# The first head pair of the prompt's attention goes ahead in the scheduler's order; batch 0's last two key pages move to other buffers

## The chip, the cores and the metric

One NeuronCore of one Trainium2 chip runs the whole program. The metric is device time in microseconds, the median of three runs. Engines are named as in the profile: PE (TensorE matmul), PEld (its weight load), DVE (VectorE), ACT (ScalarE), POOL (GpSimd) and SP (SyncE). SP, ACT and POOL also issue DMAs.

## What is computed

One inference step of one decoder layer, for a prompt of 512 tokens and for a sample group of 8 sequences of 4 tokens, all in float32:

```python
z  = RMSNorm(x) @ W_in            # columns: RWKV-7 group | FoX attention group | conv group
x += concat(RWKV7(z_A), FoX(z_B), Conv(z_C)) @ W_out
x += CrossAttn(RMSNorm(x), memory K/V)
x += ConvGLU_FFN(RMSNorm(x))
```

Two parts of it meet in the change. **FoX attention of the prompt**, 8 heads of 64, causal:

```python
s = q @ k.T * scale + c[:, None] - c[None, :]     # c: cumulative log forget gates
p = softmax(where(kpos <= qpos, s, -inf));  o = p @ v
```

**FoX attention of the sample**: each of the 8 sequences attends to 2048 cached positions, in 16 pages of 128 that a page table scatters over a pool, plus its own 4 tokens. Keys and values of all heads of one sequence are 8 MB, which the kernel reads by indirect DMAs.

## The kernel before

The program is written in a framework that schedules it: the Python code yields instructions in a program order, every instruction has a priority (its place in that order, moved ahead by `tc.high_priority(n)` by n places), and the scheduler picks, for each engine, the ready instruction with the best priority by its own model of time. What comes out is a fixed queue for each engine, worked off in order on the chip. Tiles come from pools; a pool with n buffers hands out a buffer when the earlier user of it is done, and pools that are opened after others are closed lie on the same storage.

The stage around the change begins at some 306 us, when the last matmul of the input projection is done, and ends at some 634 us, when the cross attention's first matmul starts. Two streams are woven in program order (line 1757), each with a weight that says how fast it advances:

- `sample_past`: for each of the 8 sequences `past_scores(b)` takes four key parts of 1 MB ("pages" below: 128 partitions of 2048 values). Each is loaded by one indirect DMA issued on POOL's queue (line 1292), transposed on DVE (line 1434, `KT`), and multiplied in 32 small matmuls into `bank_s`. After four of them a softmax follows on DVE and ACT. Two sequences later `past_values(b)` takes four value parts of 1 MB.
- `rest`: what is left of the RWKV recurrence, `recurrence_end`, then `prompt_attention` woven with `side_work` (`memory_norm`, `conv_module`), then `memory` (the prompt's memory keys and values, weights `w_xk` and `w_xv`) and `out_prompt` (the output projection).

Key pages live in the pool `wraw` (two buffers, tile `w_raw`), value pages in the pool `fpg` (three buffers, tile `page`). `memory_norm` also takes two tiles from `fpg` (`gain, more = page(), page()`, line 1510). Its first row block uses half of `more` as scratch, its second is loaded into the other half. `fpg` lies on the storage that the input projection's activations held until then.

Batch 0's first two key pages are fetched early, before the stage (lines 1300 and 1301, list `first_keys`). The other two are fetched by `past_scores(0)` when a buffer of `wraw` is free, that is after the first and the second transpose.

`attend(j)` (line 1365) does one pair of heads. For each of four row blocks i it forms scores of both heads in two PSUM banks (three banks `bank_r` go around), adds the causal mask `tri` and takes the minimum on DVE (line 1359, into `S0` and `S1`), and takes the exponential on ACT (line 1381). Then come transposes of `S`, the values' matmuls and the scaling (line 1403), which is the last step of a pair. `tri` is made in `recurrence_end` (lines 1355 and 1356) with its ordinary priority. `tri`, `S0` and `S1` lie in a pool `at` that is opened when the recurrence's storage has been given back; eight stores of the sample's RWKV state (line 1117, from the recurrence's `S0`, issued by SP) still read some of that storage.

`urgent(steps, ahead)` (line 350) runs every step of a stream with `tc.high_priority(ahead)`.

Of the kernel before, what the change touches and what calls it, by code (L numbers as in the profile page):

```python
# [154 lines left out]
def hybrid_step(tc, A):  # L155
# [3 lines left out]
    def pool(name, bufs=1, stack=es, right=False, **kw):  # L159
        return stack.enter_context(tc.tile_pool(name=name, bufs=bufs, side="right" if right else "left", reuse_waits="tile", **kw))  # L160
# [15 lines left out]
    def acopy(out, in_):  # L176
        nc.scalar.copy(out, in_)  # L177
# [7 lines left out]
    def mm(out, lhsT, rhs, start=True, stop=True):  # L185
        pinned(nc.tensor.matmul(out, lhsT, rhs, start=start, stop=stop, skip_group_check=True))  # L186
# [27 lines left out]
    def tr(out, in_, p0=0):  # L214
        k = in_.shape[0]
        pinned(nc.tensor.transpose(out=out, in_=in_, identity=ident[p0:p0 + k, p0:p0 + k]))  # L216
# [133 lines left out]
    def urgent(steps, ahead):  # L350

        while True:
            with tc.high_priority(ahead):
                step = next(steps, None)
            if step is None:
                return
            yield step
# [6 lines left out]
    pg = pool("pg", 2, psA, space=PSUM)  # L364
# [11 lines left out]
    def xb():  # L376
        return px.tile([128, 512], F32, name="bank_x")
# [912 lines left out]
    def four_pages(t, cache, b, pg):  # L1290

        nc.gpsimd.indirect_dma_start(out=t, out_offset=None, in_=A[cache][0].rearrange("n (k j) h d -> (n k) (j h d)", j=4),
                                     in_offset=bass.IndirectOffsetOnAxis(ap=kidx[:, 4 * b + pg: 4 * b + pg + 1], axis=0),
                                     bounds_check=32 * NPHYS - 1, oob_is_err=True)
        return t
# [4 lines left out]
    with tc.high_priority(1500):  # L1300
        first_keys = [four_pages(wraw.tile([128, 2048], F32, name="w_raw"), "cache_fox_k", 0, pg) for pg in range(2)]
# [56 lines left out]
    def add_min(out, a, b, least):  # L1358
        nc.vector.tensor_tensor_reduce(out=out, in0=a, in1=b, scale=1.0, scalar=3e38, op0=ADD, op1=MINO, accum_out=least)
# [5 lines left out]
    def attend(j):  # L1365
        q, k = yF[:, j], kF[:, j]
        st = at2.tile([128, 2, 3, 4], F32, name="st")

        S = [at.tile([128, OFF[4]], F32, name=f"S{r}") for r in range(2)]
        for i in range(4):  # L1370
            n = 128 * (i + 1)
            two = [xb() for _ in range(2)]
            for ps, ro in zip(two, HALF):
                mm(ps[:, :n], q[ro, i * 128: (i + 1) * 128], k[ro, :n], True, False)
            for r, ps in enumerate(two):
                co = slice(64 * r, 64 * r + 40)
                mm(ps[:, :n], e8[co, 2 * j + r: 2 * j + r + 1].broadcast_to([40, 128]), cum[co, :n], False, True)
            for r, ps in enumerate(two):
                o = S[r][:, OFF[i]: OFF[i] + n]
                add_min(o, ps[:, :n], tri[:, SEQ - n:], st[:, r, 0, i: i + 1])  # L1380
                act(out=o, in_=o, func=AF.Exp, scale=-1.0, bias=st[:, r, 0, i: i + 1], accum_out=st[:, r, 1, i: i + 1])
            yield 0.35 * (i + 1) + 0.4
        nc.vector.reciprocal(st[:, :, 2], st[:, :, 1])
        PT = [at.tile([128, OFK[4]], F32, name=f"PT{r}") for r in range(2)]
        for kb in range(4):
            for r in range(2):
                ps = xb()
                for i in range(kb, 4):
                    tr(ps[:, (i - kb) * 128: (i - kb + 1) * 128], S[r][:, OFF[i] + kb * 128: OFF[i] + (kb + 1) * 128])
                anycp(PT[r][:, OFK[kb]: OFK[kb + 1]], ps[:, : 512 - 128 * kb])  # L1390
                yield 0.11 * (4 - kb)
        ps = xb()
        for r, ro in enumerate(HALF):
            for i in range(4):
                mm(ps[ro, i * 128: (i + 1) * 128], st[:, r, 2, i: i + 1].broadcast_to([128, 64]), ident)
        yield 0.9
        rinv = at.tile([128, SEQ], F32, name="rinv")
        acopy(rinv, ps)
        ps = xb()
        for kb in range(4):  # L1400
            for r, ro in enumerate(HALF):
                mm(ps[ro, kb * 128:], vF[:, kb, j * 128 + r * 64: j * 128 + (r + 1) * 64], PT[r][:, OFK[kb]: OFK[kb + 1]], kb == 0, kb == 3)
        vtt(out=yF[:, j, :SEQ], in0=ps, in1=rinv, op=MUL)
        yield 2.2
# [11 lines left out]
    def page():  # L1416
        return fpg.tile([128, 2048], F32, name="page")
# [2 lines left out]
    nc.vector.memset(Pn, 0.0)  # L1420
    ysm = fs1.tile([128, 8, NS], F32, name="ysm")

    held = {}
    def past_scores(b):
        g, b4 = b // 4, b % 4
# [73 lines left out]


    def prompt_attention():
        for j in range(4):
            yield from attend(j)


# [102 lines left out]
    def rest():  # L1608
        nonlocal xTs, kTm, vm, bw
        yield from woven((recurrence, 48.0), (conv_work, 48.0))  # L1610
        recurrence_end()
        mk = pool("mk", 1, mks, True)
        kTm = mk.tile([128, 8, NMEM], F32, name="kTm")
        vm = mk.tile([128, 2, D], F32, name="vm")
        mraw = pool("mraw", 2, m2s, True)
        at_once[0] = 1
        for step in woven((prompt_attention(), 42.0), (side_work(), 33.0, 0.1)):
            yield step * 1.44
        ats.close()
        cvs.close()  # L1620
        wsplit[0] = pool("msp", 2, m2s, True)
        wslot[0] = Slots((mraw, 2), (pool("more", 3, m2s, True), 3))
        yield from memory()
        bw = pool("bwb", 2, m2s, True)
        xTs = residual_places()
        for step in out_prompt():
            yield step * 2.16
# [601 lines left out]
```

## Time and profile before

| | |
|---|---|
| median of 3 runs | 1235.73 us (1229.98 to 1239.14) |
| profiled execution, its own time | 1240.32 us |
| its span | 1238.6 us |
| PE busy, PEld busy | 1147.9 us (93%), 988.1 us (80%) |
| DVE, ACT, POOL busy | 809.7 us (65%), 501.0 us (40%), 282.1 us (23%) |
| moved by DMA | 173.81 MB |

The span is the time from the first to the last instruction. Busy shares are means over stages with different limits; what the change can do is read from the stage of 306 to 634 us alone.

### The profile page before, as it was taken

Reading aid. Unit: us, or ns where it says so; the run is one execution under the profiler, and the core shown is the slowest. Engines: PE = TensorE matmul, PEld = TensorE weight load, DVE = VectorE, ACT = ScalarE, POOL = GpSimd, SP = SyncE. Lnnn points to the kernel's source line nnn. Section 1 sums busy time; section 2 is a strip of 40 time slices with the busy share of each in tenths; the row PEclk is TensorE's granted clock in tenths of the full one; section 3 lists DMA queues with packets and bytes.
Section 4 is the critical chain, followed back from the end, with each engine's and each line's share of the span. In section 5 each row is a group of like instructions: output and inputs, shape, how many; then the busy total and the mean of one; then the engine's idle time right before and its main releaser. Section 6 shows DMA issues by size and latency. Waiting matters only on the chain.

```text
span 1238.6 us, 24738 instructions
## 1 busy us (share of the span) xinstructions
PE 1147.9 (93%) x10354; PEld 988.1 (80%) x10354; DVE 809.7 (65%) x1516; ACT 501.0 (40%) x1001; POOL 282.1 (23%) x318
## 2 busy tenths in 40 slices
PE   6889989999589998989989979999999999999997
PEld 6888878787354555965578746999999999999997
DVE  4698999877668666883256855567777326767522
ACT  5454553342255445534343223355444223444321
POOL 1253430033333332212322420021111001111120
PEclk9999989999698998999989989999999999999999
DMA  7221120122886879887435561233231332322241
GB/s 241 62 68 46 60 86 2 45 84 90 297 294 225 347 290 340 311 283 245 178 112 162 182 216 31 87 113 103 69 102 57 88 107 82 102 93 68 80 121 44
DMA packets 125952, 173.81 MB, mean 140 GB/s; under 512 B 9349, under 2 KB 107413, under 8 KB 117640
## 3 DMA queue, kind: packets, MB, share of 16 engines
q1 hardware_dynamic: 84624, 71.29, 18.7%
q0 software_dynamic: 15056, 84.28, 18.6%
q10 hardware_dynamic: 26160, 16.66, 4.8%
q8 instruction: 81, 1.33, 0.5%
q14 instruction: 31, 0.25, 0.1%
HBM read 164.54 MB, written 7.88 MB: 139 GB/s over the span
## 4 chain that ended last, share of the span: by engine, by line
PE 66%; DVE 12%; issue 9%; ACT 6%; DMA 4%; POOL 3%; POOLq 0%; SPq 0%; DVEq 0%; ACTq 0%
PE bank_g L186 39%; PE bank_d L186 7%; PE bank_r L186 7%; PE bank_s L186 4%; PE bank_v L186 3%; PE bank_a L186 2%; PE bank_r L216 2%; DVE w_lo L247 1%; DVE four L891 1%; PE bank_t L216 1%; DMA w_raw<-in_w_xk_dram 1%; DMA page<-in_cache_fox_v_dram,kidx 1%; ACT w_lo L1470 1%; ACT w_hi L177 1%; DMA w_raw<-in_w_in_dram 1%
## 5 line engine op out<-in xcount | busy, mean ns | idle before, releaser
L186 PE MATMUL bank_g<-four,w_hi 128*128 128x272 f32 (+1 forms) x1536 | 278.1, 299 | 0.7 <-DVE xT L1795 0.6
L177 ACT CAST w_hi<-w_raw 128x1024 fp32r<-128x1024 f32 (+3 forms) x149 | 140.5, 946 | 256.2 <-PE bank_g L186 183.6
L186 PEld LDWEIGHTS bank_g<-four,w_hi 128*128 128x128 f32 x1536 | 221.4, 188 | 10.6 <-issue 5.8
L247 DVE TENSOR_TENSOR w_lo<-w_raw,w_hi 128x1024 fp32r<-128x1024 f32 (+3 forms) x149 | 163.5, 1099 | 83.4 <-ACT w_hi L177 79.8
L186 PE MATMUL bank_g<-four,w_lo 128*128 128x272 f32 (+1 forms) x768 | 171.5, 298 | 0.0
L186 PE MATMUL bank_g<-act_h,w_hi 128*128 128x272 f32 (+2 forms) x400 | 123.2, 308 | 7.6 <-ACT w_hi L177 3.7
L186 PEld LDWEIGHTS bank_g<-four,w_lo 128*128 128x128 f32 x768 | 121.9, 189 | 3.1 <-issue 0.6
L186 PE MATMUL bank_g<-act_l,w_hi 128*128 128x272 f32 (+2 forms) x400 | 120.9, 302 | 0.0
L186 PE MATMUL bank_g<-act_h,w_lo 128*128 128x272 f32 (+2 forms) x400 | 120.7, 302 | 0.0
L2140 POOL TENSOR_SCALAR ysm<-HS,vec 128x32 f32<-128x32 f32 x44 | 41.9, 953 | 255.2 <-ACT HS L177 255.2
L186 PEld LDWEIGHTS bank_g<-act_h,w_hi 128*128 128x128 f32 x400 | 78.1, 195 | 12.2 <-ACT w_hi L177 4.1
L1434 DVE STREAM_TRANSPOSE KT<-w_raw 128x2048 f32<-128x2048 f32 x32 | 73.6, 2300 | 11.0 <-DMA w_raw<-in_cache_fox_k_dram,kidx 10.1
L186 PEld LDWEIGHTS bank_g<-act_l,w_hi 128*128 128x128 f32 x400 | 78.2, 195 | 3.2 <-issue 2.3
L186 PEld LDWEIGHTS bank_g<-act_h,w_lo 128*128 128x128 f32 x400 | 77.8, 195 | 3.1 <-issue 1.6
L186 PE MATMUL bank_d<-four,w_hi 128*128 128x272 f32 x384 | 80.0, 304 | 0.0
L186 PE MATMUL bank_g<-in_l,w_hi 128*128 128x272 f32 x352 | 73.4, 290 | 0.0
L186 PE MATMUL bank_g<-in_h,w_hi 128*128 128x272 f32 x352 | 73.4, 290 | 0.0
L186 PE MATMUL bank_g<-in_h,w_lo 128*128 128x272 f32 x352 | 73.2, 289 | 0.0
L186 PEld LDWEIGHTS bank_d<-four,w_hi 128*128 128x128 f32 x384 | 63.4, 197 | 1.1
L2132 DVE TENSOR_TENSOR up<-bank_g,tot 128x544 f32<-128x544 f32 x44 | 31.8, 722 | 44.7 <-PE bank_g L186 44.6
L186 PE MATMUL bank_s<-KT,w_hi 128*32 128x128 f32 x1024 | 43.8, 305 | 17.7 <-DVE mss L234 9.2
L186 PE MATMUL bank_d<-four,w_lo 128*128 128x272 f32 x192 | 57.8, 301 | 0.0
(623 smaller groups left out, 2386.0 us busy)
## 6 DMA issues: line engine op xcount, KB each, us to landing
w_raw<-in_w_up_dram SPq DMA_DIRECT2D x20, 1024.0 KB, 5.2
w_raw<-in_w_down_dram SPq DMA_DIRECT2D x16, 704.0 KB, 4.6
w_raw<-in_w_in_dram SPq DMA_DIRECT2D x10, 1024.0 KB, 10.2
w_raw<-in_cache_mem_k_dram SPq DMA_DIRECT2D x16, 512.0 KB, 4.9
sV<-in_cache_mem_v_dram POOLq DMA_DIRECT2D x12, 512.0 KB, 6.0
w_raw<-in_w_xk_dram ACTq DMA_DIRECT2D x8, 512.0 KB, 16.4
w_raw<-in_w_xv_dram ACTq DMA_DIRECT2D x8, 512.0 KB, 11.6
w_raw<-in_w_out_dram ACTq DMA_DIRECT2D x8, 512.0 KB, 11.1
```

Source lines behind the costliest of these rows:

```text
L177: nc.scalar.copy(out, in_)
L186: pinned(nc.tensor.matmul(out, lhsT, rhs, start=start, stop=stop, skip_group_check=True))
L216: pinned(nc.tensor.transpose(out=out, in_=in_, identity=ident[p0:p0 + k, p0:p0 + k]))
L247: tt(out=l, in0=src, in1=h.bitcast(F32), op=SUB)
L891: vstt(out=yp, in0=U[:, m, w: w + SEQ], scalar=w_tap, in1=yp, op0=MUL, op1=ADD)
L1434: nc.vector.transpose(out=KT, in_=K)
L1470: anycp(PT[to, j].rearrange("p (g h q) -> p g h q", g=4, q=TS), ps[po].rearrange("p (g h a q) -> p a g h q", g=4, a=4, q=TS)[:, p4])
L2132: vtt(out=two(x[:, 2:]), in0=ev2(ps), in1=two(rstd), op=MUL)
L2140: nc.gpsimd.tensor_scalar(out=ysm, in0=H[:, 2:6, 1:], scalar1=w[2], scalar2=b, op0=MUL, op1=ADD)
```

## The change

Two edits. The first takes two more key pages of batch 0 into `first_keys`, in tiles of `fpg` (the value pages' places) and with 1500 places of priority. `past_scores(0)` then finds all four pages in the list, so the first fetches into `wraw` that follow are those of batch 1. The second runs `attend(0)`, the first two heads, with 1200 places of priority; `attend(1)` to `attend(3)` are as before.

```diff
@@ -1420,6 +1420,8 @@
     nc.vector.memset(Pn, 0.0)
     ysm = fs1.tile([128, 8, NS], F32, name="ysm")
 
+    with tc.high_priority(1500):
+        first_keys += [four_pages(page(), "cache_fox_k", 0, pg) for pg in range(2, 4)]
     held = {}
     def past_scores(b):
         g, b4 = b // 4, b % 4
@@ -1499,7 +1501,8 @@
 
 
     def prompt_attention():
-        for j in range(4):
+        yield from urgent(attend(0), 1200)
+        for j in range(1, 4):
             yield from attend(j)
```

## Rows read from the trace of the kernel before

**Rows 1.** Busy time by stretch: us, then each engine, PE clock, DMA share, GB/s.

```profile
306.00:313.60 7.60, 5.39 (x87) 4.17 (x86) 7.35 (x8) 2.98 (x5) 4.75 (x6) 1.00 0.95 279
313.60:322.80 9.20, 0.03 (x6) 0.02 (x3) 3.97 (x6) 0.94 (x5) 2.03 (x2) 0.57 0.99 335
322.80:340.00 17.20, 13.68 (x115) 7.95 (x116) 13.11 (x33) 4.43 (x16) 5.25 (x5) 0.60 0.77 272
340.00:363.00 23.00, 20.34 (x203) 11.63 (x201) 15.40 (x25) 14.08 (x41) 7.45 (x8) 0.88 0.78 281
...
452.00:466.00 14.00, 11.13 (x137) 8.60 (x136) 7.26 (x14) 4.87 (x8) 2.85 (x4) 1.00 1.05 366
466.00:530.00 64.00, 60.59 (x553) 50.56 (x554) 49.85 (x80) 33.32 (x67) 15.62 (x13) 0.95 0.93 315
...
600.00:634.00 34.00, 28.96 (x257) 19.00 (x258) 14.90 (x25) 12.62 (x26) 6.13 (x6) 0.98 0.29 109
```

**Rows 2.** Timeline of PE, 306 to 330 us: start, us, instruction, idle before.

```profile
306.29 0.48 PE L186 MATMUL bank_r<-four 64*128 64x128 f32 x2
...
310.43 1.08 PE L186 MATMUL bank_s<-KT,w_hi 128*32 128x128 f32 x32 [0.51 <-DVE KT L1434]
312.53 1.08 PE L186 MATMUL bank_s<-KT,w_hi 128*32 128x128 f32 x32 [1.02 <-DVE KT L1434]
322.79 1.94 PE L186 MATMUL bank_s<-KT,w_hi 128*32 128x128 f32 x32 [9.17 <-DVE mss L234]
326.73 1.94 PE L186 MATMUL bank_s<-KT,w_hi 128*32 128x128 f32 x32 [2.00 <-DVE KT L1434]
328.59 2.08 PE L186 MATMUL bank_s<-NX,sel 128*128 128x512 f32 x2
```

**Rows 3.** Timeline of DVE, 308 to 336 us.

```profile
308.00 4.48 DVE L1434 STREAM_TRANSPOSE KT<-w_raw 128x2048 f32<-128x2048 f32 x2
...
320.42 2.31 DVE L1434 STREAM_TRANSPOSE KT<-w_raw 128x2048 f32<-128x2048 f32 x1 [5.13 <-DMA w_raw<-in_cache_fox_k_dram,kidx]
...
324.12 0.38 DVE L1355 MEMSET tri<- 128x384 f32 x1
...
326.81 0.29 DVE L1359 CUSTOM_DVE_ANT_0 S<-bank_r,tri 128x128 f32<-128x128 f32 x1
...
329.10 0.29 DVE L1359 CUSTOM_DVE_ANT_0 S<-bank_r,tri 128x128 f32<-128x128 f32 x1 [1.99 <-DMA w_raw<-in_w_xk_dram]
...
332.97 2.31 DVE L1434 STREAM_TRANSPOSE KT<-w_raw 128x2048 f32<-128x2048 f32 x1
```

**Rows 4.** Timeline of POOL, 308 to 315 us.

```profile
308.36 0.51 POOL L786 DMA_DIRECT2D out_dram<-vs  x1 [4.48 <-DVE vs L765]
...
311.15 1.14 POOL L1292 DMA_INDIRECT w_raw<-in_cache_fox_k_dram,kidx  x1 [0.17 <-issue]
...
313.43 1.18 POOL L1292 DMA_INDIRECT w_raw<-in_cache_fox_k_dram,kidx  x1 [0.30 <-issue]
```

**Rows 5.** Timeline of ACT's DMA queue: the first load into a page buffer.

```profile
306.18 0.34 ACTq L1511 DMA_DIRECT2D page<-in_g_mem_dram  x1
```

**Rows 6.** View of the cached keys' tensor, its DMAs, all 32.

```profile
DMA to landing us min/median/max: 5.7/7.9/11.3
```

**Rows 7.** View of tile S, 300 to 345 us: the state stores.

```profile
L1117 SPq DMA_DIRECT2D out_dram<-S x8: 596/666/1112, 309.3 to 314.8; - x8
...
DMA to landing us min/median/max: 14.7/14.7/14.7
```

**Rows 8.** View of line 1403: a pair's last step, duration, first and last start.

```profile
L1403 DVE TENSOR_TENSOR four<-bank_r,rinv x4: 691/692/692, 367.3 to 452.5; 128x512 f32<-128x512 f32 x4
```

**Rows 9.** Chain of waits, 440 to 626 us.

```profile
452.53 12.44 DMA w_raw<-in_w_xk_dram
...
612.92 1.35 PE bank_v L186 x16
...
615.83 3.99 PE bank_g L186 x17
```

## Prediction

> **What bounds the kernel now.** I first cut the stage that the change touches into stretches [rows 1]. The reader is to see that PE has work nearly all the time, except at the start: from 313.6 to 322.8 us it is busy for 0.03 of 9.2 us, and in the next 17.2 us it runs at a mean granted clock of 0.60, that is mostly at 1.2 GHz. The DMA engines are full in that hole (share 0.99) and full again from 452 to 530 us (1.05, 0.93).
>
> Then PE's timeline [rows 2]: two key pages are multiplied at 310.43 and 312.53, then nothing for 9.17 us, then the third page at 322.79 and the fourth at 326.73, each 1.94 us where the first two took 1.08. The row puts the 9.17 us down to a small DVE instruction; DVE's timeline [rows 3] says what came before it: the transpose of the third key page starts at 320.42, after DVE idled 5.13 us for that page's DMA. POOL's timeline gives the reason [rows 4]: the third and fourth page are issued at 311.15 and 313.43, when the first two transposes (308.00, 4.48 us long) have freed a buffer. So the start of the stage waits for two pages that had no place to land.
>
> The first head pair is not what PE lacks: its first score matmuls run at 306.29 [rows 2], before any key page. It stands still until the mask `tri` exists, made on DVE at 324.12 and used first at 326.81 [rows 3]. The last step of the pair is at 367.3 [rows 8].
>
> At the far end both streams stop together: the last value page is multiplied at 612.92, the last of the output projection at 615.83 [rows 9]. So the stage is shortened only by what both gain, or by work moved into idle time.
>
> **The change part by part.** *Two key pages in the value pages' places.* Their storage is free when the projection's last matmul is done; a load into such a buffer is issued at 306.18 today [rows 5], and POOL idles 4.48 us before 308.36 [rows 4], so the two issues of 1.1 us each fit there and cost nothing. If POOL's queue has them behind the waiting store instead, they go out at 308.9 and 310.0; still 2.3 to 3.4 us earlier than now. With the median landing of 7.9 us [rows 6] the third page arrives at about 314 (312 to 320 by the shortest and longest landing and both issue times), so its transpose ends at 316.5 and the fourth page's at about 319. Batch 1's first two pages take the issue slots at 311.15 and 313.43. They land later than the pages there do now, by the 2 MB put ahead of them: at 335 GB/s [rows 1] some 6 us, less what starts early, so 321 to 328. Both can be transposed before the mask's first use at 326.81 or soon behind it.
>
> What this is worth: two page groups more on PE by about 330, 2 x 1.94 us at the clock of that time, and 2 x 2.31 us of DVE [rows 2, 3] moved from a stretch where DVE is busy 13.11 of 17.2 us [rows 1] into its idle time. I take 4 us. The hole itself stays for the most part: between 313.6 and 330.6 PE had 1.94 + 1.94 + 2.08 = 6.0 us of work, and has 9.9 then.
>
> The clock: PE's 13.68 busy us at 0.60 and 20.34 at 0.88 [rows 1] would take 13.68 x 0.40 + 20.34 x 0.12 = 7.9 us less at full clock. With some 7 us of idle left in the hole, I expect the clock to fall as it does now, and take 0 of this; the bounds are 0 and 7.9.
>
> *What the two pages push.* `memory_norm` keeps its first page buffer and gets its second one after the third page's transpose (316.5 for a load issued about 308 now); the first value page waits for the fourth's. Both are needed late: the memory's projection starts behind the head pairs, whose last step is at 452.5 [rows 8], and no value page is multiplied before the first batch's softmax is done. I cost this at 0; without that cover it is one landing, 7.9 us, on the sample's stream. ACT, which works in order, holds the scratch use of that buffer at its head until 316.5; queued behind it are the head pair's exponentials, which wait for the mask at 326.81 anyway.
>
> *The head pair's priority.* It can't bring the mask earlier, since that is made outside `attend` at the ordinary priority. Nor can it bring the second head's tile earlier: the add into `S` at 329.10 waits 1.99 us for a DMA [rows 3]. The row names a weight load that touches other storage; the state stores, whose last issue is at 314.8 and whose landing took 14.7 us [rows 7], end at 329.5, and they read storage that the tile now gets. So what the priority moves is what follows: on DVE, key transposes of 2.31 us (one at 332.97 [rows 3]) and a softmax stand between the pair's rows now, and go behind them. The pair lasts 41 us, 326.81 to 368.0 [rows 3, 8]; with its row adds, copies and banks first I estimate 10 to 15 us less, worked out from two to three transposes and one softmax moved behind it. The sample's stream is later by about as much, minus the two pages it has in hand. PE's work is the same. The prompt's stream then asks for `w_xk` earlier; today the chain waits 12.44 us for it from 452.53 [rows 9], in a stretch where the DMA share is 1.05 [rows 1]. The bounds are a gain of that 12.4 us and a loss of one page interval, 7.9 us; I take a gain of 2, near the lower end, since the pages that fill the DMA engines there are still to be moved.
>
> **Sum.** 4 + 0 + 2 = 6 us off the profiled execution's 1240.3 us gives 1234.3. That execution lies 4.6 us above the median of the runs shown (1235.7), so by the median it is 1229.7, and I predict 1230.
>
> **Rivals.** *Given back.* The start gains, but the stretch from 452 to 530 us moves its bytes at 315 to 366 GB/s with the DMA engines full [rows 1] and sets when both streams go on. Against it: the rest of the stage has free DMA time (0.77 in 322.8 to 340). Time: 1236, between 1232 and 1240.
>
> *The hole closes.* Pages land near 312 and batch 1's near 319, PE never stands still for long and keeps its clock: 9.2 us of idle and 7.9 us of slow clock go, 17 us, so 1219 (1213 to 1223). Against it stands the DMA share of 0.99 in the hole. The Trainium skill speaks for it (TensorE: Matmul & The Clock Gate, HAM oscillation): a wait for a DMA between groups of matmuls lets the clock fall, and the next group starts cold. The rows here agree that the 1.94 us groups follow the 9.17 us wait; whether a shorter wait spares the clock no row shows.
>
> *The priority blocks DVE.* This is the slower side. If the queue of DVE has the add into `S1` ahead of batch 1's transposes, DVE stands at it until the state stores land at about 329, and batch 1's pages and batch 0's softmax wait behind. The rows of the pair follow first, so batch 1's first transpose goes from 332.97 to about 345, 12 us; with the 4 us won it is 8 us later on the sample's stream, which ends with the other one, so 1244; with a value page's landing lost as well (7.9 us), 1252. It decides if the mask is on DVE before about 322 while the stores land no earlier. Rule and row: the Trainium skill (DMA: Bandwidth & Descriptors, Queues, rings and completion order) has each DMA engine take turns between the queues, so pages on POOL's queue would not hold SP's stores back by their full bytes; were it one line for all, the 2 MB would put the stores at 335 and this rival at about 1250. No row here tells the two apart.
>
> **How the numbers follow.** Chances: forecast 0.38 (1224 to 1235), given back 0.23, hole closes 0.22, blocks DVE 0.17. The edits move the whole queue of each engine over 300 us of a stage, so I leave each case some us of scatter. Eight in ten lie in 1212 to 1247: the low end is the closed hole with part of the `w_xk` wait, the high end the blocked DVE at its middle. One per cent is 12.4 us, about what a measurement tells here (three runs spread over 0.7%): faster means below 1223.4. That is nearly all of the closed hole and the forecast's low edge, 0.29. Slower means above 1248.1, most of what the blocked DVE holds above its middle, and a share for it of scatter: 0.13. Within 1%: 0.58.
>
> **What would show it.** In the profile after: two indirect key loads into `page` at 306 to 310 us; the third page's matmuls at 316 to 318 and not 322.8; four more groups in `bank_s` before 331, not two; the mask still at 322 to 328; the add into `S1` at about 329; line 1403 first at 352 to 358; the granted clock still at half over most of 316 to 332. I am wrong if the third page lands after 320 (the issue was not the limit), if the mask moves by more than 5 us, if the first pair is not done by 360, or if PE's idle time after 340 us changes by more than 8 us, which no row of before foretells.

## The result and the profile after

The changed kernel takes 1243.16 us (median of 19 runs, 1230.46 to 1248.7) where the kernel before took 1233.74 beside it (19 runs, 1229.41 to 1242.15): ratio 1.0058, 95% interval 1.0037 to 1.0078. By the ratio it is slower by some 7 us, where the prediction had 1230. (All ratios here are taken over the fast executions, and are not the quotient of two medians.) The profiled execution has a span of 1242.0 us (1238.6 before).

I read the stretches first, cut as in [rows 1] (columns as there).

```profile
313.60:322.80 9.20, 6.00 (x105) 4.41 (x98) 6.74 (x6) 0.00 (x0) 3.78 (x4) 0.50 1.03 386
322.80:340.00 17.20, 8.24 (x57) 4.37 (x59) 7.82 (x22) 4.97 (x18) 2.01 (x2) 0.60 0.79 274
340.00:363.00 23.00, 18.69 (x184) 10.89 (x183) 16.44 (x31) 13.42 (x40) 5.14 (x5) 0.81 0.56 194
452.00:466.00 14.00, 7.03 (x82) 5.85 (x81) 3.01 (x3) 0.20 (x1) 2.37 (x2) 0.83 1.04 388
466.00:530.00 64.00, 58.18 (x525) 48.58 (x526) 49.48 (x82) 30.11 (x59) 18.09 (x14) 0.93 0.90 311
```

PE has 6.00 us of work in the stretch where it had 0.03, and 8.24 in the next where it had 13.68: by 340 us it has done 14.24 us against 13.71. What the early pages filled opened again right behind them, and ACT did nothing at all for the first 9.20 us (0.00). From 340 to 363 PE does 1.7 us less, at the far end 4.1 and 2.4 us less. DVE's timeline names the new hole (compare [rows 3]).

```profile
315.43 0.38 DVE L1355 MEMSET tri<- 128x384 f32 x1
315.73 2.25 DVE L1436 STREAM_TRANSPOSE KT<-page 128x2048 f32<-128x2048 f32 x1
318.36 2.31 DVE L1436 STREAM_TRANSPOSE KT<-page 128x2048 f32<-128x2048 f32 x1 [0.38 <-DMA page<-in_cache_fox_k_dram,kidx]
...
323.24 2.31 DVE L1436 STREAM_TRANSPOSE KT<-w_raw 128x2048 f32<-128x2048 f32 x1 [2.46 <-DMA w_raw<-in_cache_fox_k_dram,kidx]
325.47 0.25 DVE L1359 CUSTOM_DVE_ANT_0 S<-bank_r,tri 128x128 f32<-128x128 f32 x1
...
334.62 0.29 DVE L1359 CUSTOM_DVE_ANT_0 S<-bank_r,tri 128x128 f32<-128x128 f32 x1 [8.53 <-DMA w_raw<-in_w_xk_dram]
335.44 2.31 DVE L1436 STREAM_TRANSPOSE KT<-w_raw 128x2048 f32<-128x2048 f32 x1
```

The two early pages do what they were to do: they are transposed at 315.73 and 318.36. The mask's first instruction comes 8.7 us earlier, its second (line 1356) at 320.59 and not at 326.59. Then DVE stands 8.53 us at the add into the second score tile (1.99 before), with batch 1's next page and the rest of the pair behind it. As before, the row names a weight load that touches other storage; by the tile's view it is the eight state stores, whose storage that tile gets (compare [rows 7]; runs 3 to 5 bear it out). The landing in that view is that of one of the eight.

```profile
L1117 SPq DMA_DIRECT2D out_dram<-S x8: 596/811/5059, 309.9 to 327.0; - x8
...
DMA to landing us min/median/max: 18.0/18.0/18.0
```

One of the eight now takes 5.06 us to issue, and two of them wait 5.7 us in sum for earlier ones to land before they go out, so the last goes out at 327.0 and not at 314.8. The add runs when they have landed. ACT's timeline shows a second hold, on another queue.

```profile
309.71 0.45 ACTq L1516 DMA_DIRECT2D page<-in_mem_prompt_dram  x1
318.60 10.84 ACTq L279 DMA_DIRECT2D w_raw<-in_w_xk_dram  x2
329.61 1.06 ACT L447 ACTIVATE page<-page 128x1024 f32<-128x1024 f32 x1 [19.69 <-DMA w_raw<-in_w_xk_dram]
331.46 0.39 ACT L1381 ACTIVATE S<-S,st 128x128 f32<-128x128 f32 x1
```

The row of 10.84 us (1.80 in the trace of before) joins two issues and the time between them. What each issue took, the view of line 279 tells, of before first and then of the change; the third row is from the waits of SP's queue:

```profile
L279 ACTq DMA_DIRECT2D w_raw<-in_w_xk_dram x2: 421/880/1340, 315.0 to 315.5; - x2
L279 ACTq DMA_DIRECT2D w_raw<-in_w_xk_dram x2: 380/384/387, 318.6 to 329.1; - x2
SPq L1117 <- DMA out_dram<-S: 5.7, 2, 3.0
```

In the change each load is issued in under 0.4 us, and ACT stands between the two from 318.99 to 329.05. The chain of waits, further down, says for what: a state store issued at 311.37 lands 17.66 us later, at 329.03, and the second load follows at 329.05. (In the trace that load and that store carry the same completion semaphore, number 116. The program's DMAs on SP and ACT go round eight such semaphores, and a DMA goes out when the earlier one with its semaphore has landed.) What stands behind the load in ACT's queue waits with it: the memory's norm (line 447) and the pair's first exponential, 6 us after its add. POOL's timeline shows what is ahead of all this: two pages of 1 MB (compare [rows 4]).

```profile
306.98 1.11 POOL L1292 DMA_INDIRECT page<-in_cache_fox_k_dram,kidx  x1 [2.51 <-PE bank_g L186]
308.40 1.02 POOL L1292 DMA_INDIRECT page<-in_cache_fox_k_dram,kidx  x1 [0.30 <-issue]
```

A pair's last step (line 1403, [rows 8]) and the chain of waits ([rows 9]) give the length of it.

```profile
L1403 DVE TENSOR_TENSOR four<-bank_r,rinv x4: 651/670/692, 372.5 to 446.6; 128x512 f32<-128x512 f32 x4
```

```profile
311.37 17.66 DMA out_dram<-S
329.05 5.49 DMA w_raw<-in_w_xk_dram
...
447.97 17.73 DMA w_raw<-in_w_xk_dram
...
620.49 3.99 PE bank_g L186 x17
```

The pair that was given priority is done 5.2 us later than before, and the first two rows of the chain are the store that held ACT and the load behind it. The fourth pair is done 5.9 us earlier, but the prompt's stream then waits 17.73 us for `w_xk` where it waited 12.44, and the output projection's end, a mark of the stage's, has moved from 615.83 to 620.49.

### The profile page after: what moved, and what is told of

Its sections match the earlier page's. It is cut to its first block, busy times and chain, and to the rows that moved or that the text cites. A ratio compares the mean times of both kernels' runs of the same rounds, so it can differ in the third digit from the quotient of the medians.

```text
span 1242.0 us, 24736 instructions
## 1 busy us (share of the span) xinstructions
PE 1145.9 (92%) x10354; PEld 990.7 (80%) x10354; DVE 809.6 (65%) x1517; ACT 500.5 (40%) x1000; POOL 283.3 (23%) x318
## 4 chain that ended last, share of the span: by engine, by line
PE 65%; DVE 12%; issue 9%; DMA 7%; ACT 5%; POOL 2%; SPq 0%; POOLq 0%; ACTq 0%; DVEq 0%
PE bank_g L186 39%; PE bank_d L186 7%; PE bank_r L186 7%; PE bank_s L186 3%; DMA page<-in_cache_fox_v_dram,kidx 2%; PE bank_a L186 2%; PE bank_v L186 2%; DMA w_raw<-in_w_xk_dram 2%; DVE w_lo L247 2%; PE bank_r L216 2%; DMA out_dram<-S 1%; DVE four L891 1%; PE bank_t L216 1%; ACT w_hi L177 1%; DMA w_raw<-in_w_in_dram 1%
## 5 line engine op out<-in xcount | busy, mean ns | idle before, releaser
L186 PEld LDWEIGHTS bank_g<-act_h,w_hi 128*128 128x128 f32 x400 | 78.3, 196 | 10.4 <-issue 3.3
L1436 DVE STREAM_TRANSPOSE KT<-w_raw 128x2048 f32<-128x2048 f32 x30 | 69.0, 2303 | 6.0 <-DMA w_raw<-in_cache_fox_k_dram,kidx 5.2
L1292 POOL DMA_INDIRECT w_raw<-in_cache_fox_k_dram,kidx x30 | 34.9, 1162 | 106.6 <-DVE KT L1436 81.7
L186 PE MATMUL bank_g<-xT,w_hi 128*128 128x256 f32 x256 | 51.0, 298 | 8.1 <-ACT sq L1574 8.1
```

What stands on the lines that cost most here:

```text
L1436: nc.vector.transpose(out=KT, in_=K)
```

## The experiments

Eighteen runs followed. The table has them all; "first pair", "fourth pair" and "stage" are the last steps of those pairs (line 1403 or its place) and the start of the cross attention's first matmul, in us from the start of the first key transpose of the stage, in each kernel's profiled execution. The ratio is to the kernel before on the same chip. "Apart" means that the second score tile lies off the stores' storage.

| kernel | ratio, 95% | first pair | fourth pair | stage |
|---|---|---|---|---|
| before | 1 | 59.3 | 144.5 | 325.3 |
| the change | 1.0058 (1.0037 to 1.0078) | 64.2 | 138.3 | 329.7 |
| 1 pages alone | 1.0044 (1.0007 to 1.0082) | 60.9 | 142.6 | 331.1 |
| 2 priority alone | 0.9974 (0.9942 to 1.0005) | 49.2 | 130.6 | 317.9 |
| 3 change, no stores | 0.9953 (0.9918 to 0.9987) | 49.3 | 134.8 | 315.6 |
| 4 change, both score tiles moved | 1.0105 (1.0057 to 1.0153) | 65.4 | 144.7 | 334.3 |
| 5 change, apart | 1.0009 (0.9986 to 1.0033) | 54.7 | 128.1 | 319.4 |
| 6 change, weight loads on SP | 0.9976 (0.9947 to 1.0006) | 60.0 | 132.3 | 317.3 |
| 7 change, apart, weight loads on SP | 0.9966 (0.9938 to 0.9993) | 56.7 | 130.6 | 317.6 |
| 8 priority, apart | 0.9929 (0.9899 to 0.9958) | 45.1 | 123.3 | 310.5 |
| 9 before, weight loads on SP | 1.0066 (1.0035 to 1.0096) | 57.6 | 142.3 | 329.0 |
| 10 before, apart | 1.0006 (0.9974 to 1.0037) | 57.1 | 141.2 | 322.1 |
| 11 priority, apart, weight loads on SP | 0.9954 (0.9923 to 0.9985) | 45.5 | 123.7 | 316.0 |
| 12 priority, no stores | 0.9996 (0.9971 to 1.0020) | 46.7 | 124.5 | 320.0 |
| 13 change, first two weight loads on SP | 1.0025 (0.9985 to 1.0065) | 60.8 | 134.6 | 323.0 |
| 14 the same, apart | 1.0043 (1.0010 to 1.0077) | 56.7 | 130.8 | 323.5 |
| 15 priority, one early page | 1.0007 (0.9979 to 1.0036) | 52.8 | 136.4 | 315.9 |
| 16 number 8 again | 0.9931 (0.9895 to 0.9968) | 45.1 | 123.2 | 313.4 |
| 17 change, apart, conv module first | 1.0162 (1.0123 to 1.0201) | 57.3 | 153.3 | 341.0 |
| 18 priority, apart, conv module first | 1.0093 (1.0055 to 1.0131) | 52.1 | 145.2 | 335.8 |

The profiled execution of before took 1240.32 us, 2 to 8 us more than the medians of before beside these runs (1232.77 to 1238.42). So a stage is compared with another changed kernel's rather than with the 325.3, and the ratio decides.

**Run 1, the pages alone, and run 2, the priority alone.**

```diff
 run 1:
-        yield from urgent(attend(0), 1200)
-        for j in range(1, 4):
+        for j in range(4):
 run 2:
-    with tc.high_priority(1500):
-        first_keys += [four_pages(page(), "cache_fox_k", 0, pg) for pg in range(2, 4)]
```

> The two early key pages alone, the head pair at its ordinary priority. Theory 'stores': the pages fill the DMA engines, the state stores land at about 334 us instead of 329, and DVE's queue has the add into S1 ahead of both transposes of batch 1, so DVE stands 8 to 10 us there and the time is 1.003 to 1.007 of before. Theory 'priority': what costs is the head pair ahead of the sample's stream; without it the pages give their 4 us, 0.996 to 0.999. Theory 'ACT': ACT is held about 10 us by its weight-load issues as in the changed kernel and the time is about 1.004, whatever the add into S1 does.

> The head pair's priority alone, key pages as before. Theory 'stores': the stores land at 329 us as before, DVE waits 2 to 3 us at the add into S1, but all eight adds of the pair stand ahead of batch 1's first transpose, which goes from 333 to about 340 us; 1.000 to 1.004. Theory 'priority': most of the 0.6% is here, 1.005. Theory 'ACT': weight-load issues take about 2 us as before, so 1.000.

The pages carry the loss; for the priority alone none of the three theories had a gain. In run 1 DVE stands 9.97 us at the same add, with no priority given to anything:

```profile
325.05 0.25 DVE L1359 CUSTOM_DVE_ANT_0 S<-bank_r,tri 128x128 f32<-128x128 f32 x1
335.29 0.29 DVE L1359 CUSTOM_DVE_ANT_0 S<-bank_r,tri 128x128 f32<-128x128 f32 x1 [9.97 <-DMA w_raw<-in_w_xk_dram]
```

In run 2 it waits 1.61 us, the stores' last issue is 6.5 us behind the first (17.1 in the change), and the first pair is done at 49.2:

```profile
333.20 0.29 DVE L1359 CUSTOM_DVE_ANT_0 S<-bank_r,tri 128x128 f32<-128x128 f32 x1
...
335.46 0.29 DVE L1359 CUSTOM_DVE_ANT_0 S<-bank_r,tri 128x128 f32<-128x128 f32 x1 [1.61 <-DMA out_dram<-S]
```

```profile
L1117 SPq DMA_DIRECT2D out_dram<-S x8: 644/694/1067, 314.8 to 321.3; - x8
```

**Run 3, the change without the eight state stores, and run 4, with both score tiles elsewhere.**

```diff
 run 3:
-            for b in range(NB):
-                load(out=A["s_rwkv"][0, b]..., in_=S0[HALF[b % 2], b // 2]...)
 run 4 (the two lines of PT, further down, go ahead of S):
+        PT = [at.tile([128, OFK[4]], F32, name=f"PT{r}") for r in range(2)]
         S = [at.tile([128, OFF[4]], F32, name=f"S{r}") for r in range(2)]
```

> The changed kernel without its eight stores of the sample's RWKV state (that output is left out). Theory 'stores': the add into S1 follows that into S0 at about 326 us without a wait, PE's idle time of 7.8 us before 335 goes, and the time falls to 0.995 to 1.000 of before. Theory 'ACT': the add comes early, but the exponentials still wait until about 330 us for ACT's weight-load issues; 1.002 to 1.005. Theory 'priority': no change, 1.005.

> The changed kernel with the tiles of the transposed weights allocated ahead of the score tiles, so that S1 lies on other storage; every queue has the same instructions in the same order but for a place or two. Theory 'stores': the add into S1 comes at about 326 us and waits under 1 us, though the stores still land at about 334; 0.995 to 1.000 of before. Theory 'ACT': add early, exponentials at 330 us or later, 1.002 to 1.005. Theory 'priority': 1.005.

Without the stores neither add waits, the first exponential follows its add by 0.44 us (329.65), and the first pair is done at 49.3, level with run 2:

```profile
329.21 0.29 DVE L1357 CUSTOM_DVE_ANT_0 S<-bank_r,tri 128x128 f32<-128x128 f32 x1
...
329.77 0.28 DVE L1357 CUSTOM_DVE_ANT_0 S<-bank_r,tri 128x128 f32<-128x128 f32 x1
```

Run 4 missed its aim: the first score tile came to lie on the stores' storage, its add waited 8.89 us, the second's followed without a wait. The wait goes with the storage, not with the tile. The kernel lost more than the change, I take it because both adds were held.

**Runs 5 to 8: the two waits taken away one by one.** In 5, 7 and 8 the second score tile goes behind the probabilities' tiles, in 6 and 7 the weight loads of the stage go out on SP's queue. Run 8 has no early pages.

```diff
 5, 7, 8:
-        S = [at.tile([128, OFF[4]], F32, name=f"S{r}") for r in range(2)]
+        S = [at.tile([128, OFF[4]], F32, name="S0")]
+        PT = [at.tile([128, OFK[4]], F32, name=f"PT{r}") for r in range(2)]
+        S.append(at.tile([128, OFF[4]], F32, name="S1"))
 6, 7:
-    wload[0] = nc.scalar.dma_start
+    wload[0] = nc.sync.dma_start
```

> The whole change, with the second head's score tile put on the storage that a later tile has in the change, so that neither score tile lies where the state stores read. Same queues, same loads. Times count from the first key transpose of the stage. Theory 'stores' (the loss is DVE standing at the add into the second score tile until the state stores have landed, which the two early pages delay): both adds run within 1 us of each other 17 to 25 us behind the start, neither waits over 2 us, the first pair's last step is by 55 us (64.2 in the change, 49.2 with the priority alone), and the ratio is 0.995 to 1.001. Rival 'ACT' (the loss is ACT standing in the issue of the w_xk loads, which takes 10.84 us where it took 1.80): the first add comes early, but the exponentials still start only behind that issue at about 23 us, the pair ends at 60 or later, ratio 1.003 to 1.006. Rival 'bytes' (the early pages only fill the DMA engines, and every later load is late): the pair may end earlier, but the w_xk wait near 450 us grows by as much, ratio 1.003 to 1.006.

> The whole change, with the stage's weight loads issued on SP's queue in place of ACT's, so that ACT is not held by their issue. The score tiles stay where the change has them. Theory 'ACT': ACT's first activation behind the loads runs at about 10 us from the start and not at 21, the exponentials follow their adds by less than 1 us, the first pair is done by 55 us, ratio 0.995 to 1.001. Theory 'stores': the add into the second score tile still waits 7 to 10 us for the state stores, the pair ends at 60 us or later, ratio 1.003 to 1.007. If the issue of the eight stores on SP is still 15 us or longer, the pages and not the weight loads fill the queues.

> The whole change with both edits: the weight loads on SP's queue, and the second score tile off the storage of the stores. 'Stores' and 'ACT' each alone: like the better of the two single edits. Both together (each wait hides the other): the single edits give little, this one gives the first pair by 50 us and a ratio of 0.990 to 0.998. 'Bytes': both waits are gone and the ratio is still 1.002 or more, with the time back in the w_xk wait and in the waits for value pages.

> The priority without the two early pages, with the second score tile off the storage of the stores. With the priority alone that add waited 1.61 us, so 'stores' has at most 2 us to give back here: ratio 0.994 to 0.998, the first pair by 48 us. If the moved tile costs something by itself (another tile comes to lie on the stores' storage), the ratio is above 0.999 and the runs with the moved tile are to be read with that cost taken off.

Run 5 takes DVE's wait away (the two adds follow each other), though the stores are no faster. The first pair gains 9.5 us and keeps it: 10.2 at the fourth, 10.3 at the end of the stage. By the ratios it is 0.5% or 6 us.

```profile
325.06 0.25 DVE L1359 CUSTOM_DVE_ANT_0 S<-bank_r,tri 128x128 f32<-128x128 f32 x1
...
325.59 0.28 DVE L1359 CUSTOM_DVE_ANT_0 S<-bank_r,tri 128x128 f32<-128x128 f32 x1
```

Run 6 gains 0.8%, but at the first pair only 4.2 us of its 12.4, and 6.4 of them come behind the fourth pair, far from the hold of ACT at the start. In it the eight stores still take 16.43 us from the first issue to the last on SP, so it is not the weight loads that hold them. The two edits don't add up (run 7). Run 8 is the fastest. It spoils the reading of run 5 twice. Against it the pages still cost 0.8% in run 5, with DVE's wait gone. And the moved tile is worth as much beside the priority alone (run 2 to 8, 0.45%), where the add had waited only 1.61 us; at the first pair, though, 4.1 us there and 9.5 here. The difference of 5.4 us is what I can put down to the 6.9 us by which the pages lengthen the wait. So my theory of that wait holds for about a third of the 15.0 us that the pages cost at the first pair (49.2 to 64.2), not for all.

**Runs 9 to 12, the controls.** Run 9 is before with the edit of run 6, run 10 before with that of run 5, run 11 is run 8 with the edit of run 6, run 12 is run 2 with the edit of run 3.

> The kernel before, with the stage's weight loads issued on SP's queue: the control for the change with the same edit (0.9976, where the change itself has 1.0058). If that edit mended a hold on ACT that only the two pages made, it is worth nothing here: ratio 0.998 to 1.002. If ACT's queue stood at weight loads all over the stage, pages or not, this run gains as much as the change did, 0.990 to 0.994, and the edit says nothing on the pages.

> The kernel before, with the second head's score tile off the storage of the state stores: the control for the runs with the moved tile. The add into that tile waited 1.99 us before, so by that wait alone the ratio is 0.997 to 1.001. Below 0.996, the moved tile is worth something of its own (the planner orders the stage anew), and the gain of the priority with the moved tile (0.9929) is not the priority's alone.

> The priority, the moved score tile and the weight loads on SP's queue, without the early pages. If the three add up, 0.989 to 0.993; the change with the last two and the pages had 0.9966. If it is no faster than the priority with the moved tile (0.9929), the loads' queue is worth nothing where no pages are early.

> The priority without the early pages, and without the eight state stores (the output s_rwkv is left out). The change without those stores had 0.9953, the priority alone with them 0.9974. Theory 'collision' (the pages cost time only by meeting the stores): without stores the pages cost nothing or gain their 4 us, so this run is 0.995 to 0.999. Theory 'bytes' (pages ahead of their time make later loads late, stores or not): this run is faster than the change without stores by 4 us or more, 0.989 to 0.992.

Moving the weight loads to SP's queue costs 0.7% in before (run 9) and gains 0.8% in the change: for run 9 neither outcome that I had written down. Beside the priority with the moved tile (run 11 against 8) it is no gain, as the second outcome there had it; the 0.25% that it loses are within the intervals. The moved tile is worth nothing without the priority (1.0006).

With the stores gone (run 12, just above the range that 'collision' had, with most of it inside its interval) the pages are worth 0.4% (0.9996 to 0.9953), 5.3 us, near the 4 us that I had estimated for them; with the stores there they cost 0.8% (0.9974 to 1.0058), 10.4 us. At the first pair it is 2.6 us without the stores (46.7 to 49.3) and 15.0 with them (49.2 to 64.2). By ratio and by first pair the collision with the stores is the cause: it decides the sign. The traces don't follow it to the end. At the fourth pair the pages cost 10.3 us without the stores (124.5 to 134.8) and 7.7 with them, so the whole gain of run 3 over run 12 lies behind that pair, where the kernels of the table differ by up to 16 us. That it equals my 4 us is luck as far as the traces tell.

**Runs 13 to 16: which hold of ACT, and the dose.** In 13 and 14 only the first two weight loads go to SP; 15 has one early page; 16 repeats run 8.

```diff
 13, 14:
-    wload[0] = nc.scalar.dma_start
+    first_two = [nc.sync.dma_start] * 2
+    wload[0] = lambda **kw: (first_two.pop() if first_two else nc.scalar.dma_start)(**kw)
 15:
-        first_keys += [four_pages(page(), "cache_fox_k", 0, pg) for pg in range(2, 4)]
+        first_keys += [four_pages(page(), "cache_fox_k", 0, pg) for pg in range(2, 3)]
```

> The whole change, with only the first two weight loads of the stage (the ones that ACT's queue stood at for 10.84 us) on SP's queue, all later ones on ACT's as in the change. Theory 'ACT's hold': the whole gain of moving all loads (1.0058 to 0.9976) comes from these two: ratio 0.993 to 0.999, and ACT's first activation of the stage at 12 to 14 us from the start and not at 21. Rival 'later loads' (the gain came from the weight loads near 450 us being issued ahead, on a queue that nothing holds): ratio 1.003 to 1.007, though ACT is free at the start.

> The same, and the second head's score tile off the storage of the state stores. If the two waits are in series (ACT's and DVE's), 0.989 to 0.995, level with the priority without the pages (0.9929) or ahead of it; if they hide each other, 0.996 to 1.001, like each alone.

> The priority with one early page in place of two. If the hold is the filling of the DMA queues by what is issued ahead of the state stores, a dose of one gives about half: the issue of the eight stores on SP between 7.2 and 17.7 us, near 12; ACT's first two weight loads between 2.0 and 10.8 us, near 6; ratio 1.000 to 1.004. If the early pages cost by what they do to the order of DVE's queue, the issues may be short and the ratio is anywhere between 0.997 and 1.006.

> The priority without early pages, with the moved score tile, once more, beside the runs above on one chip: 0.990 to 0.996, as in the first run of it (0.9929). It is the fastest version so far; it stands if the interval stays below 1.

Line 447 runs 13.4 us from the start in run 13 (21.3 in the change), and the ratio falls between what the two theories had: what the edit frees on ACT is worth 3.4 us at the first pair. Whether the rest of run 6's gain came with the later loads, the intervals don't tell. Beside the moved tile it is worth nothing (run 14 is no better than run 5, and outside both outcomes written down). But ACT is not free in either run. The next DMA on its queue, the second load of the memory's rows (line 1517 in run 14), stands there until another state store has landed:

```profile
329.55 0.33 ACTq L1517 DMA_DIRECT2D page<-in_mem_prompt_dram  x1
329.93 0.29 ACT L220 ACTIVATE rsq<-mss,few 128x1 f32<-128x1 f32 x1 [6.48 <-DMA out_dram<-S]
```

The same wait is 5.07 us in run 13, 5.71 in run 6 and 3.64 in run 7, and the first exponential of run 14 starts at 330.60, 4.3 us after its add. So no run with the pages and the stores has taken the stores' hold off ACT, and the two holds can't be called independent.

The dose works on the stores: one early page gives 13.54 us from the first issue of the eight stores to the end of the last, between 7.19 (run 2) and 17.66 (the change), a longest single issue of 4.19 us between 1.07 and 5.06, a wait of the second add of 4.64 us between 1.61 and 8.53, and a ratio between theirs. ACT's two weight loads missed what I had written: 1.02 us and not near 6. ACT stood 7.6 us even so, ahead of them, and the first went out at 326.84, when a state store had landed; it is the landing that holds ACT, not the cost of an issue.

```profile
L1117 SPq DMA_DIRECT2D out_dram<-S x8: 596/746/4186, 311.3 to 323.2; - x8
```

Run 16 confirms run 8. It is the version to keep: the priority, no early pages, the second score tile off the stores' storage, 0.7% faster than before, and 1.3% faster than the change. Its pairs:

```profile
L1404 DVE TENSOR_TENSOR four<-bank_r,rinv x4: 691/691/692, 354.1 to 432.2; 128x512 f32<-128x512 f32 x4
```

**Runs 17 and 18: is the rest the memory's norm?** With the pages ahead, line 447 waits 11.65 us for the norm's rows (run 14) and not 4.62 (run 16), and the norm's steps then fall between the pair's.

```diff
     def side_work():
-        yield from memory_norm()
         yield from conv_module()
+        yield from memory_norm()
```

> The whole change with the second head's score tile off the storage of the state stores (1.0009 so far), and the conv module ahead of the memory's norm in the side work. Theory 'memory norm pushed': with two pages ahead of it the memory's rows land 11.7 us after their issue and not 4.6, so the norm's steps (square, scale, eight transposes in a score bank, their copies) fall between the first pair's rows on ACT, DVE and PE, while without the pages they run ahead of the mask; with the norm out of the way the first pair's last step comes at 48 us or earlier (54.7 before this edit, 45.1 without the pages) and the ratio at 0.991 to 0.997. Rival 'stream order' (the sample's groups, ready earlier, take DVE and PE ahead of the pair): the pair still ends at 52 to 56 us, ratio 0.999 to 1.003.

> The control: the priority without early pages, with the moved score tile (0.9929 and 0.9931), and the conv module first. By 'memory norm pushed' the norm was no hindrance here: pair at 44 to 47 us, ratio 0.991 to 0.996. If it gains by 0.4 per cent or more too, the order of the side work is a gain by itself and the run above says less.

These two failed as a test. The order costs 1.6% by itself (run 18), and the norm was not out of the way: ACT stood 6.37 us at its line 447 in the middle of the pair's exponentials.

```profile
329.42 0.39 ACT L1383 ACTIVATE S<-S,st 128x128 f32<-128x128 f32 x1
336.27 1.06 ACT L447 ACTIVATE page<-page 128x1024 f32<-128x1024 f32 x1 [6.37 <-DMA page<-in_mem_prompt_dram]
```

## Why the prediction was wrong

**The step that failed: what the pages push, costed at 0.** I followed the storage that the two pages take and asked who wants it next. What they pushed were the transfers issued right behind them on other queues. I had the DMA share of 0.99 in that stretch [rows 1] and used it to delay batch 1's pages, but not the stores and the memory's rows, which go through the same engines. The stores' end I had taken over from [rows 7], 329.5; in the change the add that waits for them runs at 334.62. (The 14.7 us in that row are those of one store, issued at 312.27; by the trace of before the last store landed at 328.68, 0.42 us ahead of the add.) Moving the tile out of that wait gives back 6 us by the ratios (run 5), and 9.5 us at the first pair, of which 5.4 can be put down to the pages; taking the stores away gives back 1% (run 3).

**The cover named for ACT was a real cover for a smaller hold.** I let the exponentials wait for the mask "anyway" until 326.81. The pages themselves brought the mask to 320.6, which I had excluded only for the priority; the first add came at 325.47, and ACT was held until 329.5, by a weight load that could not go out before a state store had landed (329.03). In before that store had landed in time, and the two loads went out at 315.0 and 315.5. So this hold too is the stores' late landing. Moving the two loads away is worth 3.4 us at the first pair (run 13); what the whole hold is worth, no run shows.

**Pages, a gain of 4 us: the landings right, the gain lost behind them.** The issues at 306.98 and 308.40 are as predicted, the two transposes end some 1.5 us later than forecast (317.98 and 320.67), and the third page's matmuls start at 318.04 (316 to 318 forecast, 322.79 before). Without the stores the pages bring 5.3 us by the ratios (runs 12 and 3), though not at the place that I had in mind. I expected four more page groups on PE before 331 and there were two: the next one runs at 336.87, since in PE's queue it stands behind scores of the pair that wait 7.83 us for DVE.

```profile
318.04 1.94 PE L186 MATMUL bank_s<-KT,w_hi 128*32 128x128 f32 x32 [2.45 <-DVE KT L1436]
...
334.97 1.01 PE L186 MATMUL bank_r<-four 64*128 64x384 f32 x1 [7.83 <-DVE st L1359]
...
336.87 2.77 PE L186 MATMUL bank_s<-KT,w_hi 128*32 128x128 f32 x44
```

The clock was at half as I said (0.50 and 0.60), so the 0 for it stands, and the hole did not close.

**Priority, a gain of 2 us: right as far as the measurement tells.** Alone it gives 3.2 us (0.9974, the interval just reaches 1), and the first pair comes 10.1 us earlier (10 to 15 forecast). That it can't bring the second head's tile earlier held too: with that tile off the stores' storage the priority is worth 8.7 us (runs 8 and 16).

**The rivals.** The slower one described what happened, DVE at the second score tile with batch 1's page behind it, and gave 1244 for it; I gave it 0.17. Its condition, a mask before 322 with stores no earlier, was met. But I hung it on the priority, and the pages meet the condition by themselves (run 1): in before DVE reaches the mask only behind the third page's transpose, which waits 5.13 us [rows 3], and with that page early the mask no longer stands behind this wait. The text even held the right number: were the engines one line for all, the stores would land at 335. The Trainium skill (DMA: Bandwidth & Descriptors, Queues, rings and completion order) let me set that aside, as the engines take turns between the queues; measured were 334.62 after and 329.10 before, so here the stores paid nearly the whole of the bytes put ahead of them, in part because two of them were issued only when earlier ones had landed. By the same section a turn is one packet, and the stores go out in rows of 256 bytes, which I passed over; no run varied their size.

Two of the signs of being wrong came: the mask moved by 6.0 us or more, and the first pair was done at 372.5 and not by 360.

*Given back* came true as well: the fourth pair is 6.2 us earlier than before, counted from the first transpose, and the rest of the stage 10.6 us longer. Of that, 5.4 us are lost in the 40 us behind the last pair (PE busy 28.27 us there, 33.72 before), where the chain waits for `w_xk`.

**What stays open.** With the second score tile moved the early pages still cost 0.8% (run 5 against 8 and 16). The first weight loads on ACT's queue alone don't make it (run 14), but in runs 5, 7 and 14 ACT still waits for a state store, and no run has the pages and the stores without that. That the memory's norm falls between the pair's steps is only argued; runs 17 and 18 could not settle it. And from the fourth pair to the end of the stage the kernels of the table take 179.5 to 195.5 us, as the order of the queues falls out; the sign change of run 6's edit (0.8% gained in the change, 0.7% lost in before) belongs there and is not explained.

## What to carry to other kernels

A load that is moved ahead into a stretch where the DMA engines are full can be paid for by whatever is issued behind it, on any queue: list those transfers, and for each the first in-order engine that stands still until it lands. Such an engine need not read or write the data. Here ACT stood because its next DMA was not let out before an earlier store on another queue had landed. When two edits come together, price each wait under each of them alone. And look where a scheduled tile lies: here the placing of one tile was worth more than the priority alone (0.45% against 0.26%). In a timeline, a row that joins several DMA issues spans the time between them; ask the line's own view what one took.

## What the runs showed of the hardware

Transfers issued on one queue delayed those issued on two others. With two pages of 1 MB issued on POOL's queue just ahead of the stores, a 64 KB store issued on SP at 311.37 took 17.66 us to land. In before a store issued at 310.05 had landed at 314.56, and one issued at 312.27, behind the page issued at 311.15 [rows 4], took the 14.7 us of [rows 7]. The memory's rows, issued on ACT, kept line 447 waiting 11.65 us in run 14, where run 16, without the pages, had 4.62.

The issue of a single store on SP's queue, mostly 0.6 to 0.9 us, took up to 1.11 us in before, up to 4.19 with one early page and up to 5.06 with two. The stretch from the first issue to the end of the eighth was 6.53, 13.54 and 17.66 us; in the last, 5.7 us of it are waits for earlier stores to land. What stands behind an issue in the queue does not start meanwhile, but work that has started goes on: in the change a load goes out on ACT's queue at 329.85 while line 447, begun at 329.61, runs for 1.06 us.

The granted clock of TensorE fell to half in some executions ahead of the stage, and in run 3 it stayed there while PE's rows stood back to back. These are the stretches of run 3:

```profile
292.00:300.00 8.00, 7.62 (x41) 3.48 (x41) 4.24 (x10) 0.00 (x0) 0.58 (x1) 0.62 0.22 82
300.00:308.00 8.00, 8.00 (x63) 5.66 (x63) 2.92 (x10) 0.84 (x4) 0.00 (x0) 0.50 0.00 1
308.00:316.00 8.00, 8.00 (x23) 4.60 (x23) 2.63 (x9) 0.70 (x2) 1.19 (x2) 0.50 0.00 0
```

In before the clock was 1.00 over 292 to 308 us with PE busy 16.00 of 16 us. Just ahead of the fall PE had stood idle for 1.39 us in run 3 (before the matmul at 292.38), and for 0.94 at the same place in before (290.19). In runs 1 to 4 that gap was 1.38 to 1.39 us and the clock fell behind it; in the other sixteen profiled executions it was 0.93 to 0.98, and the clock fell behind it in one of them (run 10). As runs 1 to 4 were made on one chip, one execution of each, the cause is not shown. The first key transpose started at 308.0 in before, at 312.09 in run 1 (clock 0.57 from 292 to 300) and at 321.69 in run 3. So up to 13.7 us of difference between two profiled executions stood ahead of the stage, and the stages have to be compared from their own start.
